# Output weights loaded into regions that the end of attention leaves, and split into slots of attention and the delta rule

## The chip, the cores and the metric

The kernel runs on one core of one Trainium2 chip. The metric is the time of one execution on the device in microseconds. The kernel before takes 645.64 us, the median of three runs (645.34 to 646.01).

The core's engines are TensorE (PE in the profile; PEld is its weight load), VectorE (DVE), ScalarE (ACT), GpSimd (POOL) and SyncE (SP), which issues nearly all transfers of this kernel.

## The reference

One decoder block on 1024 tokens of width 1024. After an RMS norm one projection feeds two groups of heads: eight heads of stick-breaking attention and four heads of a gated delta rule. Both results are normed by head, gated, joined and multiplied by one output weight; the residual is added and the result normed again.

```python
h = rmsnorm(x, norm1_w[layer])
proj = jnp.einsum('btd,de->bte', h, w_in[layer])
sb_q, sb_k, sb_v, sb_z, g_q, g_k, g_v, g_z, g_b, g_a = jnp.split(proj, split_idx, axis=-1)
...
o_sb = rmsnorm(o_sb.transpose(0, 2, 1, 3), sb_norm_w[layer]).reshape(b, t_len, SB_WIDTH)
o_sb = o_sb * jax.nn.silu(sb_z)
...
o_gdn = rmsnorm(o_gdn.transpose(0, 2, 1, 3), gdn_norm_w[layer]).reshape(b, t_len, GDN_WIDTH)
o_gdn = o_gdn * jax.nn.silu(g_z)
...
mixed = jnp.concatenate([o_sb, o_gdn], axis=-1)
x = x + jnp.einsum('bte,ed->btd', mixed, w_out[layer])
...
return rmsnorm(x, final_norm_w)
```

Rows 0 to 511 of `w_out` belong to the attention's half of `mixed`, rows 512 to 1023 to the delta rule's half.

## The kernel before, in words

Every float32 product is made of three products of rounded parts: an operand is split into a high half (a rounded copy, made by ACT) and a low half (what the rounding left, made by DVE or POOL), and high x high, high x low and low x high are added in PSUM (`mm3`).

**What sets the order.** The kernel is written as generators, called streams. A planner (`Model`, `interleave`) runs them against estimated costs while the program is built. Whenever the planned TensorE has nothing left, the ready stream of lowest number takes its next step, and what it records is appended to TensorE's order. The operations of the other four engines are put in the order in which the planner would start them: of those whose inputs are there, the one with the lowest priority value (`OUT_WEIGHTS` = -1 goes first, then `DELTA` = 0, `WEIGHTS` = 2, `BANK` = 5, `WINDOW` = 10, `OUTPUT` = 12, `RESULT` = 20). On the chip each engine then goes through its list strictly in that order. The planner counts for a 512 KB row 1.10 us before a transfer begins, 1.64 us for its bytes and 1.50 us until it has landed (`start`, `cost`), and a stream that waits for it goes on another 0.90 + 0.07 + 0.45 us later (`HOPS`, `TO_PE`, `SLACK`). Every operation goes through one recording helper, so all lines of the profile read L358; the groups are told apart by the names of their tiles.

**The stages around the change.** Attention runs head by head in four windows of 256 queries. In the last head, window w reads the region `sgw` of fixed memory (`sg1` 4 KB per partition, `sg2` 6 KB). A window makes its scores (from `q2`, `kh`, `kl`, with running products in `cc`), which sets `s7w`, then transposes and splits them (into `ahl`) and multiplies with `v2a`, which sets `e7w` and stores the result to `o_s`. The delta rule runs beside it: a chain of small steps (DVE `v`, `state` and `xct`, ACT `vr`) whose results go to `og_s`, and whose end sets `g`. The projections fill TensorE in between (stream number 100). The last of them are the gates z4 to z7 and z0 to z3, each in two halves of 512 columns: a PSUM bank `pp` (there are two), a sigmoid by ACT (`zs`), a product by DVE (`zt`, two buffers, shared under the tag `kt`) and a store to `gate_s`, which has the lowest priority. The end of the projections sets `proj`.

**The output weights (lines 1386 to 1422).** The output weight has eight rows of 128 x 1024 float32, 512 KB each. `weights_of` loads a raw row (`wor`), and splits it when it has landed: ACT makes the high half (`woh`) with the head norm's gain as scale, DVE the low half (`wol`). Two rows are in flight; the third load follows the split of the first. `out_weights` waits for `g`, closes the delta rule's pool, opens a pool `f0` in its place and makes weights 4 to 7 there, with the raw rows in three buffers that they share with the x rows of the first three blocks (tag `xr`). `out_weights_attention` waits for `proj`, closes the pool of the projections' input, opens `f1` there and makes weights 0 to 3 in it, with two raw buffers; then it loads the final norm's row `fnw`.

**The output stage.** For each block of 128 tokens, `enter_delta` (line 1446) loads the delta rule's result and gate into one of four buffers `kq` (`mgf` in the profile) and DVE scales it in four steps; it starts when pool `f0` is open, gate z7 is done and weights are there (`len(wts) > 1`). `prepare` (line 1472) turns a block by TensorE, multiplies it by the gate (DVE `mf`) and splits it (ACT `mh`, POOL `ml`; three buffers). `products_delta` multiplies it by weights 4 to 7, in two halves of 12 matmuls, each in a `pp` bank, and DVE adds the bank to the x row (`xr<-pp,xr`), which empties the bank; block b's end sets `db`. `enter_x` loads the x rows: the first three blocks into `f0`, the rest into `f1` once that is open. `enter_attention` (line 1513) does for the attention's blocks what `enter_delta` does, with the head norm (ACT `sq`, DVE `ssb`, POOL `rsb`, DVE `mgf<-mgf,rsb`); it waits for `f1`, for weight 3 and for the last delta input. `products_attention` follows the last delta block, and after each block ACT, DVE and POOL do the final norm (`yj`, `sy`, `ry`, `xr<-pc,fnw`, `xr<-po,fnw`) and SP stores the result.

Of the kernel before, what the change touches and what calls it, by code (L numbers as in the profile page):

```python
# [22 lines left out]
SBH = 8  # L23
# [12 lines left out]
OUT_WEIGHTS, DELTA, WEIGHTS, BANK, WINDOW, OUTPUT, RESULT, DECAYS = -1, 0, 2, 5, 10, 12, 20, 25  # L36
# [437 lines left out]
def block(tc, xT_d, x_d, n1_d, wE_d, wQ_d, wC_d, conv_d, alog_d, dtb_d, mixw_d, wo_d, fnw_d, out_d):  # L474
    nc = tc.nc
    ck = Model({"V": nc.vector, "A": nc.scalar, "G": nc.gpsimd, "P": nc.tensor, "S": nc.sync})
    V, A, G, TE, S = ck.V, ck.A, ck.G, ck.P, ck.S

    with ExitStack() as top:
        top.enter_context(tc.manual_schedule(engines={mybir.EngineType.PE}))  # L480

        def open_pool(name, space="SB", ctx=top, before=(), **kw):
            if space != "SB":
                kw["space"] = getattr(bass.MemoryType, space)
            return Pool(ck, ctx.enter_context(tc.tile_pool(name=name, bufs=1, **kw)), space, before)

        fx = Fixed(ck, nc, {**{f"sg{w}": (2048 * (w + 1), 1) for w in range(4)}, "o2": (1024, 1), "kq": (4096, 4)})
# [19 lines left out]
        mixw = cst.tile([P, NK], F32, name="mixw")  # L507
# [32 lines left out]
        at_ = open_pool("att", side="right")  # L540
# [140 lines left out]
        for b in range(NB):  # L681
            xr = s0.tile([P, T], F32, tag="xr", bufs=5, name="xr")
# [295 lines left out]
        def delta_load():  # L978
            yield lambda: "dec" in flags
            for h in range(GH):  # L980
                for g in range(2):
                    u = 2 * h + g
                    gst[h, g] = {}
                    half = "" if g else ".0"
                    yield lambda: u < 4 or f"c{u - 4}" in flags
                    if u > 3:
                        yield flags[f"c{u - 4}"]
                    kq = fx.tile([P, 4, 2, P], F32, "kq", "kq")
                    ts = slice(512 * g, 512 * g + 512)
# [300 lines left out]
        def attention_values():  # L1290
            yield lambda: "v1" in flags and "dec" in flags
            for h in range(SBH):
                yield lambda: h == 0 or f"e{h - 1}3" in flags
                hd["v", h] = v2 = at_.tile([P, NB, P], F32R, tag="v2a", name="v2a")
                flags[f"va{h}"] = S.dma_start(v2.bitcast(F32), v_s[:, :, h].rearrange("b s u d -> s b (u d)").bitcast(F32))
# [90 lines left out]
        wts = {}  # L1386
        pools = {}

        def weights_of(pool, ks, tag, bufs):
            ks = list(ks)  # L1390
            raws = {}

            def load(k):
                r = pool.tile([P, D], F32, tag=tag, bufs=bufs, name="wor")
                raws[k] = r, S.dma_start(r, wo_d[k * P:(k + 1) * P, :])

            for k in ks[:2]:
                load(k)
            for n, k in enumerate(ks):
                w, landed = raws[k]  # L1400
                yield landed
                wh, wl = [pool.tile([P, D], F32R, name=f"wo{c}{k}") for c in "hl"]
                A.activation(wh, w, AF.Copy, scale=mixw[:, k:k + 1])
                wts[k] = wh, wl, V.scalar_tensor_tensor(wl, w, mixw[:, k:k + 1], wh.bitcast(F32), ALU.mult, ALU.subtract)
                if n + 2 < len(ks):
                    load(ks[n + 2])

        def out_weights():
            yield lambda: "g" in flags
            gdn_ctx.close()  # L1410
            pools[0] = open_pool("f0", before=gd.ops())
            flags["pool0"] = True
            yield from weights_of(pools[0], range(4, 8), "xr", 3)

        def out_weights_attention():
            yield lambda: "proj" in flags and "pool0" in flags
            proj_ctx.close()
            pools[1] = open_pool("f1", before=px.ops(), side="right")
            flags["pool1"] = True
            yield from weights_of(pools[1], range(4), "wr", 2)  # L1420
            fnw = wts["fnw"] = pools[1].tile([P, D], F32, name="fnw")
            S.dma_start(fnw, fnw_d.partition_broadcast(P))

# [20 lines left out]
            return pools[0].tile([P, D], F32, tag="xr", bufs=3, name=name) if b < 3 else pools[1].tile([P, D], F32, tag="yr", bufs=5, name=name)  # L1444

        def enter_delta():
            yield lambda: "pool0" in flags and "z7" in flags and len(wts) > 1
            f0 = pools[0]
            for b in range(NB):
                yield lambda: fx.room("kq")  # L1450
                mg, mx, gt = block_inputs()
                S.dma_start(mx, og_s[b].rearrange("p h d -> p (h d)"))
                S.dma_start(gt, gate_s[4:8, :, b * P:(b + 1) * P].rearrange("k e t -> e k t"))
                ck.hold(mg)
                for g in range(GH):
                    gs = slice(g * P, (g + 1) * P)
                    r = V.tensor_scalar(mx[:, gs], mx[:, gs], rsg[:, g, b:b + 1], None, ALU.mult)
                ready["in", b, 1] = mg, gt, r
                yield
# [3 lines left out]
        def enter_x():  # L1463
            yield lambda: ("in", 0, 1) in ready
            for b in range(NB):
                yield lambda: b < 3 or "pool1" in flags
                xs_[b] = block_tile(b, "xr")
                S.dma_start(xs_[b], x_d[b * P:(b + 1) * P, :])
                ck.hold(xs_[b])
                yield  # L1470
# [62 lines left out]
        def products_attention():  # L1533
            yield lambda: f"d{NB - 1}" in flags
            for b in range(NB):
# [3 lines left out]
                for got in product(b, 0, parts):  # L1539
# [43 lines left out]
        pre = Stream(delta_pre(), 0.7, DELTA + 0.7)  # L1583
        interleave(ck, lambda: ps.room("pz", 4),
                   [Stream(delta_scan(), 0, DELTA), Stream(delta_solve(), 0.5, DELTA + 0.5), Stream(delta_substitute(), 0.6, DELTA + 0.6),
                    pre, Stream(delta_load(), 0.4, DELTA + 0.4), Stream(attention(), 9.995, WINDOW), Stream(attention_values(), 9.99, WINDOW), Stream(out_weights(), 9, OUT_WEIGHTS), Stream(out_weights_attention(), 9.25, OUTPUT + 1), Stream(enter_x(), 9.31, OUTPUT), fill,
                    Stream(enter_delta(), 9.3, OUTPUT), Stream(prepare(1), 9.2, OUTPUT), Stream(products_delta(), 101, OUTPUT),
                    Stream(enter_attention(), 9.1, OUTPUT - 3), Stream(prepare(0), 9.05, OUTPUT - 2), Stream(products_attention(), 102, OUTPUT - 1.5)])

# [37 lines left out]
```

## Time and profile before

| | |
|---|---|
| median of three runs | 645.64 us (645.34 to 646.01) |
| profiled execution | 647.36 us, its span 645.0 us, granted TensorE clock 0.998 |
| busy share of the span | PE 98%, PEld 84%, DVE 68%, ACT 61%, POOL 53% |
| last head's windows 1, 2, 3 issue the store of their result | 502.0, 508.8, 515.5 us |
| delta rule issues its last store | 521.5 us |
| raw rows of the output weights issued | 523.5 to 567.8 us |
| their low halves begun | 530.9 to 577.8 us |
| products with the output weights (first to last) | 542.9 to 638.3 us |
| DMA share, 500 to 520 us, 521 to 540 us, 540 to 545 us | 0.22, 0.81, 1.06 |

Times are microseconds from the start of the span unless ns is written. A line of the timeline gives start, duration, engine, operation, the tile written, the tiles read and the shapes; in brackets stands the time for which the engine was idle before it, and what it waited for. A group's line ends with its count, its busy time, the mean time of one, and the idle time before its members. SPq is SyncE's queue: such a line is the issue of a transfer, not the transfer. The ends of matmuls are modelled: their starts are what is exact, so a pace is read from start to start.

### The profile page before, as it was taken

To read this page: it belongs to the slowest core of one execution; us is meant where nothing else is said; L and a number is where in the kernel's file an instruction comes from. 1 tells how busy PE (TensorE), PEld (TensorE's weight loads), DVE (VectorE), ACT (ScalarE), POOL (GpSimd) and SP (SyncE) were. 2 spreads that over 40 slices of the span, in tenths; PEclk is the share of its full clock that TensorE was granted. 3 is DMA by queue.
4 is the path that set the end of the run, shared out by engine and by line. 5 is a ranking of instruction groups with operands and counts; after the bars stand their busy time and mean duration, and the time that the engine had idled before them with its cause. 6 is when DMAs were issued, how large, how long until landed. Compare 5 with 4: busy or idle time off the path is not lost.

```text
span 645.0 us, 11378 instructions
## 1 busy us (share of the span) xinstructions
PE 633.7 (98%) x3816; PEld 540.5 (84%) x3816; DVE 435.6 (68%) x810; ACT 392.6 (61%) x943; POOL 340.6 (53%) x429
## 2 busy tenths in 40 slices
PE   8999999999999999999999999999999999999996
PEld 7889988988888888888888788888888887888785
DVE  4359985133776797776877677667869527486874
ACT  5665467553876677856877766757578533222653
POOL 0125142964978487773569596477626131224742
PEclk9999999999999999999999999999999999999999
DMA  8968235886286352656254583444512259962323
GB/s 294 303 245 305 86 131 162 313 286 229 81 262 189 99 172 81 202 182 185 71 169 125 158 274 84 123 146 117 185 52 73 79 191 332 357 197 65 99 99 130
DMA packets 96633, 111.80 MB, mean 173 GB/s; under 512 B 28544, under 2 KB 61504, under 8 KB 96576
## 3 DMA queue, kind: packets, MB, share of 16 engines
q1 hardware_dynamic: 96288, 110.89, 52.2%
q8 instruction: 30, 0.49, 0.3%
q14 instruction: 27, 0.22, 0.1%
q10 hardware_dynamic: 288, 0.20, 0.1%
HBM read 76.03 MB, written 35.03 MB: 172 GB/s over the span
## 4 chain that ended last, share of the span: by engine, by line
PE 53%; POOL 3%; issue 2%; DVE 2%; DMA 1%; ACT 0%; POOLq 0%; SPq 0%
PE pp L358 34%; PE pz L358 13%; PE po L358 4%; PE pc L358 2%; DMA vt<-g_s 1%; POOL sgf L358 1%; POOL rsb L358 1%; POOL tt L358 0%; DVE xr L358 0%; POOL ac L358 0%; DVE cc L358 0%; POOL wel L358 0%; DVE ahl L358 0%; POOL ml L358 0%; POOL ry L358 0%
## 5 line engine op out<-in xcount | busy, mean ns | idle before, releaser
L358 PE MATMUL pp<-xh,weh 128*128 128x512 f32 x360 | 146.0, 406 | 0.0
L358 PE MATMUL pp<-xh,wel 128*128 128x512 f32 x360 | 141.2, 392 | 0.0
L358 PE MATMUL pp<-xl,weh 128*128 128x512 f32 x360 | 140.5, 390 | 0.0
L358 POOL TENSOR_TENSOR sgf<-sgf,cc 128x128 f32<-128x128 f32 (+3 forms) x64 | 77.3, 1210 | 48.0 <-DVE cc L358 46.7
L358 POOL TENSOR_TENSOR wel<-wer,weh 128x512 fp32r<-128x512 f32 x48 | 62.1, 1298 | 68.2 <-ACT weh L358 66.4
L358 PEld LDWEIGHTS pp<-xh,wel 128*128 128x128 f32 x360 | 67.5, 188 | 15.1
L358 PEld LDWEIGHTS pp<-xl,weh 128*128 128x128 f32 x360 | 67.8, 188 | 11.7
L358 PEld LDWEIGHTS pp<-xh,weh 128*128 128x128 f32 x360 | 67.7, 188 | 11.6
L358 DVE TENSOR_TENSOR_SCAN cc<-pz,step 128x384 f32<-128x384 f32 (+2 forms) x64 | 53.4, 847 | 13.7 <-ACT pz L358 7.5
L358 DVE TENSOR_TENSOR ahl<-pz,ahl 128x512 fp32r<-128x512 f32 (+1 forms) x80 | 50.0, 631 | 11.9 <-ACT ahl L358 11.5
L358 ACT ACTIVATE ahl<-pz 128x512 fp32r<-128x512 f32 (+1 forms) x80 | 44.0, 563 | 17.7 <-PE pz L358 17.4
L358 ACT ACTIVATE sgf<-pz,rs 128x384 f32<-128x384 f32 (+3 forms) x96 | 52.9, 593 | 1.5 <-PE pz L358 1.1
L358 PE MATMUL pp<-woh,mh 128*128 128x512 f32 (+2 forms) x132 | 52.1, 395 | 1.2 <-DVE xr L358 1.2
L358 ACT ACTIVATE pz<-pz,ns 128x384 f32<-128x384 f32 (+3 forms) x96 | 52.2, 577 | 0.0
L358 PE MATMUL pp<-woh,ml 128*128 128x512 f32 (+2 forms) x132 | 50.9, 385 | 0.0
L358 PE MATMUL pp<-wol,mh 128*128 128x512 f32 (+2 forms) x132 | 50.6, 384 | 0.0
L358 PE MATMUL po<-ahl,v2a 128*128 128x512 f32 (+1 forms) x160 | 49.0, 401 | 0.0
L358 POOL TENSOR_TENSOR ac<-ac,pre 128x512 f32<-128x512 f32 x24 | 30.9, 1291 | 30.8 <-ACT pre L358 24.2
L358 POOL TENSOR_TENSOR ml<-mf,mh 128x512 fp32r<-128x512 f32 x16 | 22.0, 1377 | 42.6 <-ACT mh L358 32.3
L358 DVE SCALAR_TENSOR_TENSOR pp<-pre,conv,pp 128x512 f32<-128x512 f32 x42 | 31.5, 749 | 18.3 <-ACT pp L358 18.0
L358 DVE TENSOR_TENSOR_SCAN cc<-pz,cc,step 128x512 f32<-128x512 f32 (+1 forms) x32 | 38.8, 1211 | 5.5 <-ACT pz L358 4.8
L358 PE MATMUL pz<-kh,q 128*128 128x384 f32 (+3 forms) x96 | 36.0, 381 | 0.2 <-DVE cc L358 0.2
(290 smaller groups left out, 1531.5 us busy)
## 6 DMA issues: line engine op xcount, KB each, us to landing
wer<-wE SPq DMA_DIRECT2D x48, 256.0 KB, 3.0
xr<-x SPq DMA_DIRECT2D x16, 512.0 KB, 7.4
g_s<-ac SPq DMA_DIRECT2D x24, 256.0 KB, 2.1
v_s<-v2e SPq DMA_DIRECT2D x16, 256.0 KB, 3.0
kqf<-g_s SPq DMA_DIRECT2D x16, 256.0 KB, 3.4
v2a<-v_s SPq DMA_DIRECT2D x8, 512.0 KB, 5.9
q<-qk_s SPq DMA_DIRECT2D x8, 512.0 KB, 4.0
kh<-qk_s SPq DMA_DIRECT2D x8, 512.0 KB, 3.9
```

What stands on the lines that cost most here:

```text
L358: ins = f(*args, **kw).ins
```

## The change

The eight raw rows no longer go through buffers of the two late pools. A new stream, `out_rows`, loads them into the fixed regions `sg1` and `sg2` in turn, in the order 4, 5, 6, 7, 0, 1, 2, 3: the first once the last head's scores are done and its window 1 is through, the second after window 2, every further one when the row before it in that region has been split. Its loads have the highest priority. `out_weights` splits rows 4 to 7 into slots that attention leaves (`kh` and `kl`; `q2` and one `cc`; the other `cc` and `v2a`; both `ahl`), two of them after the scores, two after the last window; it no longer waits for the delta rule. `out_weights_attention` opens `f0` when the delta rule is done and splits rows 0 to 3 there, with a low priority. `out_rest` opens `f1` when the projections are done, as before, and loads the final norm's row after the second delta block. `enter_delta` no longer waits for weights.

```diff
-        def weights_of(pool, ks, tag, bufs):
-            ks = list(ks)
-            raws = {}
-
-            def load(k):
-                r = pool.tile([P, D], F32, tag=tag, bufs=bufs, name="wor")
+        raws = {}
+
+        def out_rows():
+            yield lambda: f"s{SBH - 1}3" in flags and f"e{SBH - 1}1" in flags
+            for n, k in enumerate((4, 5, 6, 7, 0, 1, 2, 3)):
+                if n == 1:
+                    yield lambda: f"e{SBH - 1}2" in flags
+                if n > 1:
+                    yield lambda: fx.room(f"sg{1 + n % 2}")
+                r = fx.tile([P, D], F32, "wor", f"sg{1 + n % 2}")
+                ck.hold(r)
                 raws[k] = r, S.dma_start(r, wo_d[k * P:(k + 1) * P, :])
-
-            for k in ks[:2]:
-                load(k)
-            for n, k in enumerate(ks):
-                w, landed = raws[k]
-                yield landed
-                wh, wl = [pool.tile([P, D], F32R, name=f"wo{c}{k}") for c in "hl"]
-                A.activation(wh, w, AF.Copy, scale=mixw[:, k:k + 1])
-                wts[k] = wh, wl, V.scalar_tensor_tensor(wl, w, mixw[:, k:k + 1], wh.bitcast(F32), ALU.mult, ALU.subtract)
-                if n + 2 < len(ks):
-                    load(ks[n + 2])
+                yield
+
+        def weight(k, wh, wl):
+            w = raws[k][0]
+            A.activation(wh, w, AF.Copy, scale=mixw[:, k:k + 1])
+            wts[k] = wh, wl, V.scalar_tensor_tensor(wl, w, mixw[:, k:k + 1], wh.bitcast(F32), ALU.mult, ALU.subtract)
+            ck.free(w)
 
         def out_weights():
+            places = [(t, 2 if t in ("cc", "ahl") else 1) for t in ("kh", "kl", "q2", "cc", "cc", "v2a", "ahl", "ahl")]
+            for n, k in enumerate(range(4, 8)):
+                yield lambda: k in raws and (n < 2 or f"e{SBH - 1}3" in flags)
+                yield raws[k][1]
+                weight(k, *[at_.tile([P, D], F32R, tag=t, bufs=m, name="wo") for t, m in places[2 * n:2 * n + 2]])
+                yield
+
+        def out_weights_attention():
             yield lambda: "g" in flags
             gdn_ctx.close()
-            pools[0] = open_pool("f0", before=gd.ops())
+            f0 = pools[0] = open_pool("f0", before=gd.ops())
             flags["pool0"] = True
-            yield from weights_of(pools[0], range(4, 8), "xr", 3)
-
-        def out_weights_attention():
+            for k in range(4):
+                yield lambda: k in raws
+                yield raws[k][1]
+                weight(k, *[f0.tile([P, D], F32R, name=f"wo{c}{k}") for c in "hl"])
+                yield
+
+        def out_rest():
             yield lambda: "proj" in flags and "pool0" in flags
             proj_ctx.close()
             pools[1] = open_pool("f1", before=px.ops(), side="right")
             flags["pool1"] = True
-            yield from weights_of(pools[1], range(4), "wr", 2)
+            yield lambda: "d1" in flags
             fnw = wts["fnw"] = pools[1].tile([P, D], F32, name="fnw")
             S.dma_start(fnw, fnw_d.partition_broadcast(P))
...
         def enter_delta():
-            yield lambda: "pool0" in flags and "z7" in flags and len(wts) > 1
+            yield lambda: "pool0" in flags and "z7" in flags
...
-Stream(out_weights(), 9, OUT_WEIGHTS), Stream(out_weights_attention(), 9.25, OUTPUT + 1), Stream(enter_x(), 9.31, OUTPUT), fill,
+Stream(out_rows(), 9.1, OUT_WEIGHTS), Stream(out_weights(), 9, OUT_WEIGHTS), Stream(out_weights_attention(), 9.25, OUTPUT + 1), Stream(out_rest(), 9.26, OUTPUT + 1), Stream(enter_x(), 9.31, OUTPUT), fill,
```

More of the change, by code (lines that the diff above doesn't have):

```diff
@@ L1585, in block @@
                    [Stream(delta_scan(), 0, DELTA), Stream(delta_solve(), 0.5, DELTA + 0.5), Stream(delta_substitute(), 0.6, DELTA + 0.6),
-                    pre, Stream(delta_load(), 0.4, DELTA + 0.4), Stream(attention(), 9.995, WINDOW), Stream(attention_values(), 9.99, WINDOW), Stream(out_weights(), 9, OUT_WEIGHTS), Stream(out_weights_attention(), 9.25, OUTPUT + 1), Stream(enter_x(), 9.31, OUTPUT), fill,
+                    pre, Stream(delta_load(), 0.4, DELTA + 0.4), Stream(attention(), 9.995, WINDOW), Stream(attention_values(), 9.99, WINDOW), Stream(out_rows(), 9.1, OUT_WEIGHTS), Stream(out_weights(), 9, OUT_WEIGHTS), Stream(out_weights_attention(), 9.25, OUTPUT + 1), Stream(out_rest(), 9.26, OUTPUT + 1), Stream(enter_x(), 9.31, OUTPUT), fill,
                     Stream(enter_delta(), 9.3, OUTPUT), Stream(prepare(1), 9.2, OUTPUT), Stream(products_delta(), 101, OUTPUT),
```

## The prediction

> **What bounds the kernel now.** I read the engine shares first, then the chain that ended last, then the waits of TensorE in the last 105 us, and last the timeline around the two places that those waits point to.
>
> ```profile
> span 645.0 us, 11378 instructions
> PE 633.7 (98%) x3816; PEld 540.5 (84%) x3816; DVE 435.6 (68%) x810; ACT 392.6 (61%) x943; POOL 340.6 (53%) x429
> ```
>
> TensorE (PE) is busy for 98% of the span. Since the ends of its matmuls are modelled, busy alone does not say that it issues as fast as it can. The chain of waits says more, because it merges matmuls that follow each other without a pause:
>
> ```profile
> 521.09 18.41 PE pp L358 x81
> ...
> 546.86 0.70 DVE xr L358
> 547.60 3.02 PE pp L358 x12
> ...
> 574.34 12.36 PE pp L358 x54
> ```
>
> 81 matmuls in 18.41 us are 227 ns each, 54 in 12.36 us are 229 ns. The first stretch is the last two gate projections, the second the output product of the delta rule. They run at one pace, though different data and a different amount of DMA traffic lie beside them. So from 521 us on TensorE works at a steady pace that this change does not touch: the same matmuls, with the same operand shapes, remain. What can be won there is its pauses, and the waits of TensorE from 540 us to the end name only these:
>
> ```profile
> PE pp L358 <- DVE xr L358: 1.2, 2, 0.8
> ```
>
> Two pauses, 1.2 us together, both waits for VectorE (DVE) to empty a PSUM bank. Their exact price comes from the starts of the matmuls around them:
>
> ```profile
> 546.43 0.39 PE L358 MATMUL pp<-woh,ml 128*128 128x512 f32 x1
> 547.60 0.50 PE L358 MATMUL pp<-woh,mh 128*128 128x512 f32 x1 [0.78 <-DVE xr L358]
> ...
> 602.92 0.39 PE L358 MATMUL pp<-woh,ml 128*128 128x512 f32 x1
> 603.72 0.47 PE L358 MATMUL pp<-woh,mh 128*128 128x512 f32 x1 [0.41 <-DVE xr L358]
> ```
>
> Start to start is 1.17 us and 0.80 us where 0.227 is the pace, so 0.94 us and 0.57 us are lost, 1.51 us together. Before 502 us the change moves nothing (its first gate opens with the attention's last windows, below). So 1.51 us is close to the most that it can win, unless the whole order behind 502 us turns out better in some way that this trace doesn't show.
>
> Here a rule of the Trainium skill speaks against my bound: "Perfetto Trace Analysis", section "Identifying the Most-Contended Engine", holds matmul busy time for a bad measure and weight-load busy time for a good one. By the 84% of the page about 103 us of the span would be headroom. The 81 matmuls without a pause show none that a move of transfers could use, so the measurement decides and the bound stands.
>
> **The loads.** The change keeps eight raw rows of 512 KB, and their eight splits, and moves them.
>
> ```profile
> L358 SPq DMA_DIRECT2D wor<-wo x8: 327/333/652, 523.5 to 567.8; - x8
> L358 ACT ACTIVATE woh<-wor,mixw x8: 1136/1140/1157, 529.7 to 573.9; 128x1024 fp32r<-128x1024 f32 x8
> L358 DVE SCALAR_TENSOR_TENSOR wol<-wor,mixw,woh x8: 1274/1280/1867, 530.9 to 577.8; 128x1024 fp32r<-128x1024 f32 x8
> DMA to landing us min/median/max: 3.2/4.2/7.0
> ...
> 497.20 2.00 POOL L358 TENSOR_TENSOR sgf<-sgf,cc 128x1024 f32<-128x1024 f32 x1 [0.40 <-DVE cc L358]
> 502.03 0.37 SPq L358 DMA_DIRECT2D o_s<-oe  x1
> 508.78 0.38 SPq L358 DMA_DIRECT2D o_s<-oe  x1
> 515.48 0.37 SPq L358 DMA_DIRECT2D o_s<-oe  x1
> ```
>
> The last head's scores end at 499.2 and its windows 1, 2 and 3 store their results at 502.0, 508.8 and 515.5. These are the gates. So row 4 can be issued at about 502, row 5 at about 509, row 6 when the split of row 4 has emptied its region (502 + 4.2 + 1.14 + 1.28, but behind row 5: 509), row 7 at about 516, and rows 0 to 3 one by one at some 4 us each from 518 on. The last split is then done near 537, where it was done at 579.7 (577.8 + 1.9). SyncE's (SP) queue gets none more to issue, 8 x 0.33 us as before. Each is moved past what SP carries from 502 to 522: the stores of the delta rule's scan, the result stores of the attention and the weight loads of the last gate tiles. A row that waits for its region holds those. I price this at nothing, because the stores' results are first wanted when the products begin (543, below), and
>
> ```profile
> 503.27 0.86 SPq L358 DMA_DIRECT2D wer<-wE  x2
> ...
> 513.21 0.62 ACT L358 ACTIVATE weh<-wer 128x512 fp32r<-128x512 f32 x1
> ...
> L358 SPq DMA_DIRECT2D og_s<-goe x8: 319/320/333, 487.3 to 521.5; - x8
> ```
>
> a gate weight issued at 503.3 is first read at 513.2; with 4.2 us to land (the raw row's time, for twice the size), the cover is 5.7 us. If that cover went, TensorE would wait for each us beyond it.
>
> **The splits.** Four of them (rows 0 to 3) leave the stretch 552 to 580: 4 x 1.14 = 4.6 us of ScalarE (ACT) and 3 x 1.28 + 1.87 = 5.7 us of DVE. Three (4 to 6) enter the stretch 500 to 520 and the others 520 to 537:
>
> ```profile
> 500.00:520.00 20.00, 20.00 (x125) 17.46 (x125) 10.03 (x24) 9.57 (x28) 4.04 (x5) 1.00 0.22 69
> ...
> L358 DVE TENSOR_TENSOR_SCAN cc<-pz,cc,step 128x512 f32<-128x512 f32 (+1 forms) x32 | 38.8, 1211 | 5.5 <-ACT pz L358 4.8
> ...
> 592.00:604.00 12.00, 11.59 (x57) 9.27 (x56) 10.36 (x16) 6.00 (x12) 9.50 (x7) 1.00 0.39 119
> ```
>
> (The windows give the busy time of PE, PEld, DVE, ACT and POOL, then clock, DMA share and GB/s.) DVE goes from 10.0 to 13.9 of 20 us there, ACT from 9.6 to 13.0. The splits of rows 4 to 7 have the highest order of all in the planner, so up to 1.3 us at a time they go ahead of the delta rule's steps (v, state, xct, vr). The scan's last store is issued at 521.5 and its product starts at 543, so 21 us of gate projections cover this: 0, unless TensorE's fixed order stands behind a step that came late. Between nothing and the price in the second rival I take nothing: the nearest row is the attention's own scan, as long, which goes between the same steps now.
>
> **What starts earlier.** The delta rule's inputs no longer wait for two split weights, and weight 3, for which the attention's inputs wait, is ready sooner:
>
> ```profile
> 528.81 0.45 SPq L358 DMA_DIRECT2D mgf<-og_s  x1
> ...
> 566.48 1.28 DVE L358 SCALAR_TENSOR_TENSOR wol<-wor,mixw,woh 128x1024 fp32r<-128x1024 f32 x1
> 567.78 0.33 SPq L358 DMA_DIRECT2D wor<-wo  x1
> ...
> 568.69 0.38 SPq L358 DMA_DIRECT2D mgf<-o_s  x1
> ```
>
> The first goes from 528.8 to about 523.5, the second (now held by SP behind the raw row, which waits for the split of 566.48) to about 555, when the second delta block is done (543.1 + 48 x 0.227 = 554). The final norm's row waits for that block too; it is first used by the first finished output block, near 600, so this costs nothing.
>
> **The first pause.** The product's second half wants a PSUM bank that the last gate tile still holds:
>
> ```profile
> 538.05 0.40 SPq L358 DMA_DIRECT2D gate_s<-zt  x1
> 543.14 0.39 PE L358 MATMUL pp<-woh,mh 128*128 128x512 f32 x1
> 543.39 0.60 ACT L358 ACTIVATE zs<-pp 128x512 f32<-128x512 f32 x1 [2.21 <-PE pp L358]
> ...
> 547.82 0.69 DVE L358 TENSOR_TENSOR mf<-pz,mgf 128x512 f32<-128x512 f32 x1 [0.28 <-POOL ml L358]
> 548.43 0.68 DVE L358 TENSOR_TENSOR zt<-pp,zs 128x512 f32<-128x512 f32 x1
> ...
> 540.00:545.00 5.00, 5.00 (x26) 4.11 (x25) 5.00 (x14) 1.23 (x2) 1.54 (x1) 1.00 1.06 379
> ...
> xr<-x SPq DMA_DIRECT2D x8, 512.0 KB, 7.5
> wor<-wo SPq DMA_DIRECT2D x2, 512.0 KB, 7.0
> ```
>
> The bank's sigmoid is done at 544.0, its second step zt runs at 548.4. Two things hold zt: its two buffers, one of which waits for a store that SP issued only at 538.05, behind loads; and the input scalings of the delta blocks, which fill DVE from 540 to 545. DMA is at its limit there (share 1.06), with eight x rows and two raw rows issued between 536 and 552. In the change the two raw rows are gone from this stretch, three x rows can be issued ahead of it with the first blocks' inputs, 5 us earlier, and the scalings come earlier too. zt then follows its sigmoid: 544.0 + 0.69 = 544.7, and the second half wants its bank at 543.1 + 12 x 0.227 = 545.9 (block transposes that move ahead of the products shift both alike). I take the whole 0.94.
>
> **The second pause.** It lies in the DVE-heavy stretch 592 to 604 (10.36 of 12 us):
>
> ```profile
> 596.70 0.15 DVE L358 TENSOR_SCALAR ssb<-ssb 128x8 f32<-128x8 f32 x1
> 599.77 1.29 POOL L358 TENSOR_TENSOR ml<-mf,mh 128x512 fp32r<-128x512 f32 x1
> 600.03 1.05 DVE L358 TENSOR_SCALAR ssb<-ssb 128x8 f32<-128x8 f32 x1
> ```
>
> With the attention's inputs 13 us earlier, their scaling no longer piles up on the first finished output blocks, so this may go. But a tiny step took 1.05 us instead of 0.15 while GpSimd (POOL) ran beside it, and that pair can meet again wherever the pile ends up. Between 0 and 0.57 I take half, 0.28.
>
> "SBUF: State Buffer", section "Who interferes with whom", of the Trainium skill states that VectorE and GpSimd share one pair of ports as an exclusive lock. The trace agrees (1.05 against 0.15). By that rule alone this pause would stay, and the sum would be 0.94.
>
> **The sum.** 0.94 + 0.28 = 1.22 us, bounds 0.94 and 1.51. The profiled execution took 647.36 us (2.36 of them outside its span), 1.72 more than the median of 645.64, so I take the difference alone to the median: 644.4, or 0.19%. A measurement of this kernel can tell about 0.2% (1.29 us, to 644.35) from no change, so this forecast lies on that line.
>
> **Rivals.** First, the pause moves and nothing is won. The saturated stretch stays: five of eight x rows (512 KB) still can't be issued until the projections end, at 543, and they alone are 2.6 MB, 7 us at the 379 GB/s reached. A DVE that waits in order for a late input holds zt or xr behind it as now. For it: DMA share 1.06. Against: 1 MB of raw rows less in that stretch. Time 645.6 (one such wait of 0.94 stays, one of 0.28 comes for the one that went).
>
> Second, slower: ACT, in order, stands in front of a raw row that hasn't landed, between 504 and 523, and TensorE's order, written for an earlier arrival, stands with it. The planner counts 4.24 us to landing and waits 1.42 more, so it decides when a landing takes over 5.66 us. The longest of the trace is 7.0: 1.34 us for each late row. With three late ones 4.0 us, less the 0.94 won: 648.7; with two, 647.4. Behind ACT's split wait vr, the copies of the attention and the gate sigmoid, for which DVE and then TensorE wait. Against it: DMA share is 0.22 there, and the 7.0 was seen at 1.06.
>
> Third, the change doesn't do what it says: the splits of rows 6 and 7 wait for the last window (515.5), and the rest for the end of the scan (522). If regions come free late, rows 0 to 3 stay in the busy stretch: 645.6.
>
> **Chances.** Forecast 0.50; of it 0.28 beyond 0.2%, since both pauses may go whole. First rival 0.26, second 0.15 (0.13 of it beyond 0.2%), third 0.05; 0.04 for a larger gain than the pauses allow. Faster 0.28 + 0.04 = 0.32; same 0.22 + 0.26 + 0.02 + 0.05 = 0.55; slower 0.13. The range goes down to both pauses (644.13) less half of the spread of the three runs (645.34 to 646.01, 0.33), 643.8, and up to one late row with nothing won, 645.64 + 1.34 = 647.0; with the 0.04 below and two or more late rows above (about 0.1), some 0.14 is left out.
>
> **What would show it.** Right: raw rows issued from 502 on, splits done before 540, zt less than 2 us behind its sigmoid, no wait of TensorE for xr near 547, the attention's first input before 560, fewer than 10.4 us of DVE in the 12 us at the first finished outputs. Wrong: a pause of TensorE between 502 and 523 that ends with ACT's vr or ahl (second rival), an unchanged 0.78 near 547 (first), splits after 545 (third), or a change of pace of the gapless matmuls from 227 ns, which would overturn the bound itself.

## The result, and the profile after

The changed kernel takes 644.59 us, the median of 20 executions (644.20 to 645.19), beside 645.83 us for the kernel before on the same chip (645.34 to 646.26). The ratio is 0.998, with a 95% interval of 0.9974 to 0.9987: 1.24 us are gone, where 1.22 were forecast. The profiled execution took 645.19 us, 2.03 of them outside its span.

The page of the changed kernel, its first part:

```profile
span 643.2 us, 11380 instructions
## 1 busy us (share of the span) xinstructions
PE 633.8 (99%) x3816; PEld 540.3 (84%) x3816; DVE 435.3 (68%) x810; ACT 392.4 (61%) x943; POOL 339.9 (53%) x429
```

Each engine carries the work that it carried before, within 0.7 us (POOL 339.9 for 340.6); the span is shorter by 1.8 us. So no engine got less to do. What went is, in the main, idle time of TensorE. Its waits from 540 us to the end name nothing any more (the list is empty), and the timeline of its matmuls shows the two places at which it paused before. The columns are start, duration, engine, line, operation and tiles:

```profile
543.03 0.63 PE L358 MATMUL pp<-wo,mh 128*128 128x512 f32 x2
...
545.60 0.39 PE L358 MATMUL pp<-wo,ml 128*128 128x512 f32 x1
545.83 0.63 PE L358 MATMUL pp<-wo,mh 128*128 128x512 f32 x2
...
602.79 0.40 PE L358 MATMUL pp<-woh,ml 128*128 128x512 f32 x1
603.02 0.40 PE L358 MATMUL pp<-woh,mh 128*128 128x512 f32 x1
...
636.51 0.28 PE L358 MATMUL pp<-woh,ml 128*128 128x192 f32 x1
```

Where 1.17 us lay between two starts there are now 0.23 (545.60 to 545.83), and where 0.80 lay there are 0.23 (602.79 to 603.02). From the first matmul of the output product to the last it is 636.51 - 543.03 = 93.48 us. The kernel before has its first there at 543.14 (shown above) and its last at 638.34:

```profile
638.34 0.28 PE L358 MATMUL pp<-woh,ml 128*128 128x192 f32 x1
```

That is 95.20 us, so the stage is 1.72 us shorter. But the two stretches don't hold the same matmuls, 456 before and 448 after. The difference is the transposes of two blocks (`pz<-step,mwf`, four to a block). Before, they stand between the products, and in the changed kernel ahead of the first of them, since the inputs come earlier. Before and after:

```profile
544.53 0.47 PE L358 MATMUL pz<-step,mwf 128*128 128x128 f32 x4
545.60 0.46 PE L358 MATMUL pz<-step,mwf 128*128 128x128 f32 x4
...
533.42 0.46 PE L358 MATMUL pz<-step,mwf 128*128 128x128 f32 x4
534.48 0.45 PE L358 MATMUL pz<-step,mwf 128*128 128x128 f32 x4
```

What leaves the stage makes the stretch ahead of it longer. Attention's store of a result just ahead of the change (`o_s<-oe`) is issued at 498.19 before and 497.35 after, and from there to the first product it is 44.95 and 45.68 us, 0.73 more. So like for like the stage is 0.99 us shorter, and from that store to the end of the span it is 1.00 (146.81 and 145.81), beside 1.24 between the medians. The other 0.84 us of the two spans' difference were lost ahead of the change, where before's profiled execution waited 1.29 us for a transfer near 366 us and the changed kernel's 0.61.

The two pauses went whole, 0.94 + 0.57 = 1.51 us, and part of this was paid back, because the pace changed. The twelve products from 543.03 to 545.83 above come every 233 ns. Over the 192 products of the delta rule's half, the starts lie 232.8 ns apart in the mean from product to product (pauses and transposes left out), where it was 228.4 before: 192 x 4.4 ns = 0.84 us. 1.51 - 0.84 is 0.67, which leaves 0.32 in pieces too small to name.

Why the first pause went is seen on DVE. Before, its timeline reads

```profile
541.63 3.47 DVE L358 TENSOR_SCALAR mgf<-mgf,rsg 128x128 f32<-128x128 f32 x12
545.09 0.69 DVE L358 TENSOR_TENSOR mf<-pz,mgf 128x512 f32<-128x512 f32 x1
```

and after

```profile
543.92 0.69 DVE L358 TENSOR_TENSOR zt<-pp,zs 128x512 f32<-128x512 f32 x1 [2.87 <-ACT zs L358]
544.53 0.87 DVE L358 TENSOR_SCALAR mgf<-mgf,rsg 128x128 f32<-128x128 f32 x4
546.03 0.69 DVE L358 TENSOR_TENSOR xr<-pp,xr 128x512 f32<-128x512 f32 x1 [0.63 <-PE pp L358]
```

The twelve input scalings that stood there are four, and DVE sat idle for 2.87 us until the sigmoid ended. `zt` comes right behind it, at 543.92 instead of 548.43, and the bank is free before the second half of the product wants it. The stretches by engine of the changed kernel (PE, PEld, DVE, ACT, POOL, then clock, DMA share and GB/s):

```profile
500.00:520.00 20.00, 20.00 (x122) 17.32 (x121) 13.00 (x27) 11.94 (x29) 4.13 (x5) 1.00 0.60 184
...
540.00:545.00 5.00, 5.00 (x24) 4.08 (x23) 1.77 (x5) 2.27 (x3) 1.61 (x2) 1.00 1.08 371
592.00:604.00 12.00, 12.00 (x59) 9.89 (x58) 8.55 (x15) 5.53 (x12) 6.30 (x5) 1.00 0.34 98
```

DVE went from 5.00 to 1.77 of 5 us at the first pause, and from 10.36 to 8.55 of 12 us at the second, while the DMA share at the first stayed as it was (1.06 and 1.08). The rows, splits and inputs, grouped by tile (duration min/median/max in ns, first and last start):

```profile
L358 SPq DMA_DIRECT2D worf<-wo x8: 328/332/448, 500.6 to 538.3; - x8
L358 ACT ACTIVATE wo<-worf,mixw x4: 1139/1142/1145, 505.8 to 522.1; 128x1024 fp32r<-128x1024 f32 x4
L358 DVE SCALAR_TENSOR_TENSOR wo<-worf,mixw,wo x4: 1273/1278/1286, 507.8 to 523.2; 128x1024 fp32r<-128x1024 f32 x4
L358 DVE SCALAR_TENSOR_TENSOR wol<-worf,mixw,woh x4: 1269/1276/1279, 528.8 to 553.4; 128x1024 fp32r<-128x1024 f32 x4
DMA to landing us min/median/max: 3.7/5.0/6.4
...
L358 SPq DMA_DIRECT2D mgf<-og_s x8: 319/354/504, 522.8 to 550.1; - x8
L358 SPq DMA_DIRECT2D mgf<-o_s x8: 319/320/320, 556.1 to 597.6; - x8
```

`wo` are the splits of rows 4 to 7, which the delta rule's half of the product reads, done at 524.5; `wol` those of rows 0 to 3, done only at 554.7.

### The profile page after: what moved, and what is told of

Its sections match the earlier page's. It is cut to its first block, busy times and chain, and to the rows that moved or that the text cites. A ratio compares the mean times of both kernels' runs of the same rounds, so it can differ in the third digit from the quotient of the medians.

```text
span 643.2 us, 11380 instructions
## 1 busy us (share of the span) xinstructions
PE 633.8 (99%) x3816; PEld 540.3 (84%) x3816; DVE 435.3 (68%) x810; ACT 392.4 (61%) x943; POOL 339.9 (53%) x429
## 4 chain that ended last, share of the span: by engine, by line
PE 91%; POOL 3%; DMA 2%; DVE 1%; issue 1%; ACT 1%; POOLq 0%; SPq 0%; ACTq 0%
PE pp L358 54%; PE pz L358 26%; PE po L358 7%; PE pc L358 3%; DMA vt<-g_s 1%; DMA o_s<-oe 1%; POOL wel L358 1%; POOL ac L358 1%; DMA n<-n 1%; DVE cc L358 0%; POOL tt L358 0%; POOL tm L358 0%; POOL sgf L358 0%; POOL xs L358 0%; DVE ahl L358 0%
## 5 line engine op out<-in xcount | busy, mean ns | idle before, releaser
L358 PE MATMUL pp<-wo,mh 128*128 128x512 f32 x128 | 40.7, 399 | 0.0
L358 DVE TENSOR_TENSOR xr<-pp,xr 128x512 f32<-128x512 f32 (+2 forms) x33 | 22.2, 672 | 19.3 <-PE pp L358 18.8
L358 PEld LDWEIGHTS pz<-step,stf 128*128 128x128 f32 x288 | 30.9, 140 | 4.8
```

Source lines behind the costliest of these rows:

```text
L358: ins = f(*args, **kw).ins
```

## The experiments

In each trace the stage from the first to the last matmul of the output product was taken, and what lies between the last matmul and the end of the span:

| kernel | ratio to before (95%) | first matmul, us | last | stage | matmuls in it | to the end |
|---|---|---|---|---|---|---|
| before | 1 | 543.14 | 638.34 | 95.20 | 456 | 6.66 |
| after | 0.9980 (0.9974 to 0.9987) | 543.03 | 636.51 | 93.48 | 448 | 6.65 |
| e1, before, delta inputs early | 1.0021 (1.0012 to 1.0031) | 541.89 | 638.61 | 96.72 | 448 | 6.94 |
| e2, before, gate stores first | 1.0073 (1.0061 to 1.0086) | 541.26 | 641.30 | 100.04 | 456 | 6.66 |
| e3, before, attention inputs early | 1.0005 (0.9997 to 1.0014) | 541.59 | 636.46 | 94.87 | 456 | 7.55 |
| e4, before, all three | 1.0019 (1.0008 to 1.0030) | 541.41 | 636.67 | 95.26 | 448 | 6.67 |
| e5, after, delta inputs late | 1.0017 (1.0009 to 1.0026) | 542.12 | 637.36 | 95.24 | 448 | 7.31 |
| e6, after, rows 0 to 3 late | 0.9988 (0.9980 to 0.9997) | 544.04 | 637.50 | 93.46 | 448 | 6.74 |
| e7, after, all rows late | 1.0033 (1.0021 to 1.0046) | 542.38 | 640.35 | 97.97 | 448 | 6.65 |
| e8, after, planner told sooner | 0.9996 (0.9987 to 1.0005) | 542.43 | 635.89 | 93.46 | 448 | 7.56 |
| e9, e8 padded | 0.9985 (0.9976 to 0.9994) | 542.93 | 636.39 | 93.46 | 448 | 7.09 |
| e10, e3 padded | 0.9995 (0.9986 to 1.0004) | 542.18 | 637.03 | 94.85 | 456 | 7.08 |
| e11, after padded | 0.9985 (0.9977 to 0.9994) | 542.93 | 636.41 | 93.48 | 448 | 7.08 |

A stage compares only with one of as many matmuls: before's 95.20 stands for 95.20 - 0.73 = 94.47 among those of 448. Without a pause the stage is 93.46 to 93.48 in five kernels (after, e6, e8, e9 and e11).

The pace falls into two groups as well. In the seven kernels that split rows 4 to 7 into slots of attention (after, e5 to e9 and e11), the products of the delta rule's half come every 233 ns (median), and in the six others every 227. The attention's half, whose weights lie in a late pool, has 227 in all thirteen. So the pace goes with the slots and costs each of the seven some 0.84 us. What it is in the slots that slows a matmul was not tested.

**Theory and rivals.** The theory was that of the prediction: two pauses, the first undone by the delta rule's inputs going early, the second by the attention's. The rivals: that one of the conditions behind these steps is the cause by itself, so that one changed line of the kernel before would win the same; and that only the loading matters. e1 to e4 change a condition of the kernel before and leave the loading as it was; e5 to e7 undo one part of the change each.

### e1: the delta rule's inputs early, rows as before

```diff
-            yield lambda: "pool0" in flags and "z7" in flags and len(wts) > 1
+            yield lambda: "pool0" in flags and "z7" in flags
...
-            yield lambda: ("in", 0, 1) in ready
+            yield lambda: ("in", 0, 1) in ready and len(wts) > 1
```

The second line, in `enter_x`, keeps the x rows where they were.

> The kernel before, with the delta blocks' inputs no longer waiting for split weights (the x rows still wait as before, since they share buffers with the raw rows). Theory (the first pause is zt, held behind the input scalings and behind a late store): the scalings go ahead of 540, but the store of the tile before is still behind loads in SP's order, so the pause near 547 shrinks without being sure to go: 645.83 less 0 to 0.94, 645.3. Rival (the raw rows' traffic between 523 and 560 makes the pause): the pause stays at 0.94 and the time at 645.8. The second pause (0.57 near 603) stays in both.

It took 646.83 us beside 645.21. Its waits of TensorE from 540 us on (us in total, times, longest):

```profile
PE pp L358 <- DVE wol L358: 1.4, 2, 1.2
PE pp L358 <- ACT woh L358: 0.3, 1, 0.3
```

and the stretch behind them, by engine as above:

```profile
546.00:550.00 4.00, 3.77 (x10) 2.67 (x9) 2.47 (x3) 1.15 (x1) 0.00 (x0) 0.57 0.96 375
```

The wait for `xr` is gone, since `zt` runs at 542.7, and against the expectation the second pause is gone too (the attention's first input leaves at 562.7, 568.7 before). In their place the product stands before its own weights: the inputs, issued at 518.7, overtake the raw rows, and the first split is at 533.4 instead of 529.7. The condition `len(wts) > 1` was there for a reason, and dropped by itself it loses. Behind the pauses the granted clock is 0.57, told of below.

### e2: stores of the last gate tiles first

```diff
+                ck.prio, prio = (OUT_WEIGHTS if i in (2, 3) else ck.prio), ck.prio
-                return S.dma_start(gate_s[i, :, hs], zt)
+                r = S.dma_start(gate_s[i, :, hs], zt)
+                ck.prio = prio
+                return r
```

> The kernel before, with the stores of the last two gate tiles at the highest priority in place of the lowest. Theory: zt gets its buffer early, but the planner still places the scalings ahead of it where they are ready; the pause near 547 goes or halves: 645.0 to 645.4. Rival (traffic): zt's buffer is no matter, 645.8. The second pause stays.

It took 649.91 us, the slowest of all. The wait for `xr` near 547 is gone, so the store that held the buffer was a cause of the first pause. But TensorE now waits at 588 to 593. The longest of its waits is

```profile
PE pp L358 <- ACT mh L358: 2.0, 1, 2.0
```

SP's timeline shows what came late:

```profile
556.13 16.92 SPq L358 DMA_DIRECT2D wor<-wo  x2
573.10 0.42 SPq L358 DMA_DIRECT2D fnw<-fnw  x1
573.57 0.42 SPq L358 DMA_DIRECT2D mgf<-o_s  x1
```

and the stretch behind the wait, by engine, is

```profile
592.00:598.00 6.00, 5.50 (x16) 4.24 (x16) 3.88 (x7) 1.89 (x3) 3.51 (x3) 0.51 0.29 92
```

SP stood at the last raw row, which waits for the split that frees its buffer, and the attention's first input left at 573.57 (568.69 before). Its block was wanted when the delta rule's products ended, near 588. So the 4.9 us by which that input came later were more than the old loading had to spare.

### e3: the attention's inputs early, rows as before

```diff
-            yield lambda: "pool1" in flags and "z3" in flags and 3 in wts
+            yield lambda: "pool1" in flags and "z3" in flags
```

> The kernel before, with the attention blocks' inputs no longer waiting for weight 3. Theory (the second pause comes from the attention's inputs piling up on the first finished blocks): first input near 560 in place of 568.7, the pause near 603 goes, the one near 547 stays: 645.83 - 0.57 = 645.3. Rival (the second pause is the port held by POOL, wherever the steps stand): the pause stays or moves: 645.8.

The first pause stays, as the one wait left shows:

```profile
PE pp L358 <- DVE xr L358: 0.8, 1, 0.8
```

The second is no longer named, but it isn't gone: the product behind a block's transposes starts 0.55 us after the first of them (601.60 and 602.15), where 0.30 is usual (544.53 and 544.83 before). So 0.25 us of 0.57 are left. The edit moved the attention's first input alone (556.9); the second left at 567.6 (569.6 before), behind the last raw row. The stage is 0.33 us shorter, which is that difference, but what follows the last matmul is 0.89 longer, so the time, 645.42 beside 645.21, shows no gain. The end is taken up at e8.

### e4: all three at once

> The kernel before with the edits of the three runs beside it together; raw rows and splits stay where they were. Theory (the gain is the two pauses, however they go): 645.83 - 0.94 - 0.57 = 644.3, as the changed kernel within 0.3. Rival (moving the raw rows is what gains, by traffic or by the splits that leave 552 to 580): 645.3 to 645.8.

Its edit is those of e1, e2 and e3 together. Its waits are, to the tenth, those of e1 (`wol` 1.4, `woh` 0.3), and the time is 645.77 (645.27 to 648.54). That is 0.56 us over the kernel before, worse than even the rival had it. With every condition set free but the rows loaded as before, nothing is won: 95.26 us of stage, 0.79 over the 94.47 that before has of the same matmuls. The rows must come first.

### e5: the changed kernel, delta inputs held back

```diff
-            yield lambda: "pool0" in flags and "z7" in flags
+            yield lambda: "pool0" in flags and "z7" in flags and len(wts) > 5
```

> The changed kernel, with the delta blocks' inputs (and with them the x rows) held until six weights are recorded, some 10 us later; the rows and splits stay as changed. Theory (a bank of the last gate tile is emptied late when the input scalings fill VectorE after 540, so both moves are needed, weights and inputs): a pause of about 0.9 near 545 returns, time 0.9 over the changed kernel, 1.2 - 0.9 = 0.3 under the kernel before (ratio 0.9995). Rival (moving the raw rows out of the traffic is enough): no pause returns, ratio 0.998 as the changed kernel.

It took 646.76 us beside 645.82. The inputs left at 528.8, the time of the kernel before, and the waits are back:

```profile
PE pp L358 <- DVE xr L358: 1.4, 2, 0.8
```

Both now lie at the start of the product (behind 544.68 and 548.96), 0.95 and 0.74 us lost, with `zt` at 549.6. These two, and not the one that was forecast, make the stage 1.76 us longer than the changed kernel's. Behind the last matmul there are 0.66 us more, of which 0.36 lie ahead of DVE's last `sy`. So early rows alone bring nothing: it took 0.94 us more than the kernel before, since the pauses are back and the slower pace stays. The gain of the early rows is that the delta rule's inputs may go early without e1's loss.

### e6: the changed kernel, rows 0 to 3 held back

```diff
-                    yield lambda: fx.room(f"sg{1 + n % 2}")
+                    yield lambda: fx.room(f"sg{1 + n % 2}") and (n < 4 or "proj" in flags)
```

> The changed kernel, with the raw rows 0 to 3 held until the projections end (near 543); rows 4 to 7 stay early. Theory (rows 0 to 3 matter only by holding the attention's inputs until weight 3 is recorded, and by their traffic): no pause near 545, but the attention's first input goes back to 565 or later and the second pause (0.3 to 0.6 near 600) returns; ratio 0.9985 to 0.999. If the held inputs come later than the products, as in the run with the store first, a pause of 2 us or more near 590 and a lower clock behind it: ratio over 1.002. Rival (rows 4 to 7 are all that counts): ratio 0.998.

It took 644.79 us beside 645.82, 0.9988 (by luck in the range of the theory, and with an interval that overlaps the changed kernel's), and no wait of TensorE is left; the stage is 93.46. The theory, by which early rows 0 to 3 undo the second pause, failed here. Their splits came at 551.7 to 570, later than in the changed kernel, and the attention's first input still left at 557.3. Early rows 4 to 7 are enough.

### e7: the changed kernel, all rows held until the scan's end

```diff
-            yield lambda: f"s{SBH - 1}3" in flags and f"e{SBH - 1}1" in flags
+            yield lambda: f"s{SBH - 1}3" in flags and f"e{SBH - 1}1" in flags and "g" in flags
```

> The changed kernel, with all raw rows held until the delta rule's scan has ended (near 522), so that they load where the kernel before loads its first four, through the fixed regions two at a time. Theory (the early weights are what lets the inputs go early): the inputs' and x rows' traffic now stands beside the rows', weights 6 and 7 come after 543, and the products wait for them as in the run with early inputs alone: 1 to 2 us of pause near 545; ratio 1.000 to 1.003. Rival (the slots, not the early time, are what counts): ratio 0.998.

It took 647.35 us beside 645.82. Its waits of TensorE:

```profile
PE pp L358 <- DVE wo L358: 1.6, 2, 0.8
PE pp L358 <- ACT wo L358: 0.4, 1, 0.4
```

and the splits of rows 4 to 7, by tile:

```profile
L358 DVE SCALAR_TENSOR_TENSOR wo<-worf,mixw,wo x4: 1281/1283/1287, 526.8 to 546.1; 128x1024 fp32r<-128x1024 f32 x4
```

The last of these splits starts at 546.1, 3.7 us after the product's first matmul, where the changed kernel has it at 523.2. The pauses lose 0.54, 1.09 and 0.98 us from start to start, and behind them the clock falls here too, to 0.61 in 547 to 551. The start of the loads inside the attention's last windows is what the change needs, and the other slots and regions win nothing by themselves.

### e8: the changed kernel, planner told that rows land 3 us sooner

```diff
-            self.at(self.dma + 1500, self.finish, op)
+            self.at(self.dma + 1500 - op.rush, self.finish, op)
...
-                yield
+                raws[k][1].rush = 3000; yield
```

`rush` is 0 for every other transfer, and 3000 ns for the eight raw rows.

> The changed kernel, with the planner told that every raw row lands 3 us sooner than it does, so ScalarE's order has each split that much earlier. The prediction's second rival says what a late row costs: ScalarE stands for 3 - 1.42 = 1.6 us in front of each row that lands as slowly as the planner otherwise counts, with the delta rule's steps behind it, and TensorE pays for those that it needs at once. Theory (the pauses of ScalarE lie under the gate projections): TensorE's order has other matmuls only until the next step of the scan, so some of it shows: 1 to 3 us over the changed kernel, ratio 1.000 to 1.003. Rival (all of it is covered): ratio 0.998.

This asks for the prediction's second rival: TensorE's order is now written for rows that come 3 us before they do. ACT waits 1.5 us for them and TensorE not once; the splits move to 503.7 to 516.8, and the stage is 93.46. A split written that much too early is covered. Yet the time is 645.47 us beside 645.82, 0.9 above the changed kernel, and the trace has it all behind the last matmul: 7.56 us instead of 6.65. The transfers of the last stores, with their us to landing at the end of each row:

```profile
out<-yf SPq DMA_DIRECT2D x1, 320.0 KB, 3.3
out<-yf ACTq DMA_DIRECT2D x1, 192.0 KB, 3.5
```

and, of the queues from 639.5 to 642.2 us, the one beside the two that carry the stores (packets, MB, share of 16 engines):

```profile
q14 instruction: 1, 0.01, 0.7%
```

One packet of 8 KB in the queue that fetches instructions lies between the packets of the last store (at 640.90, the store from 639.8 to 642.1). In e3, the other kernel whose last stores took 3.3 and 3.5 us, it is the same (at 641.46). In all the rest they took 2.4 and 2.6, and no fetch lies there.

### e9, e10 and e11: the same kernels, padded

To move the fetches without touching the work, six tiny instructions were put at the start of each of DVE, POOL and ACT, with values that no later step uses:

```diff
+        [(nc.vector.memset(root, 0.5), nc.gpsimd.memset(ns8, 0.0)) for _ in range(6)]
+        [nc.scalar.activation(rs8, ns8, AF.Copy) for _ in range(6)]
         V.memset(root, 0.5)
```

> The kernel of e8 with six tiny instructions more on each of DVE, ACT and POOL at the very start (under 1 us, before the first product), which move the place at which an engine's next piece of instructions is fetched. Theory: the 0.9 us by which e8 ended later than the changed kernel is the fetch that fell inside its last store; moved out of it, that store lands in 2.4 to 2.6 us instead of 3.3 to 3.5, the tail from the last matmul to the end goes from 7.56 to about 6.65, and the ratio from 0.9996 to about 0.998. Rival: the tail has nothing to do with the fetch; it stays near 7.5 and the ratio near 0.9996, or rises by what the padding costs.

> The kernel of e3 with the same padding. Theory: tail from 7.55 to about 6.65, ratio from 1.0005 to about 0.9992, so that the second pause alone is worth its 0.5 us. Rival: tail and ratio unchanged.

> The changed kernel with the same padding. Theory: its last store, which no fetch touched, stays so if the fetch that stood 3 us ahead of it moves further ahead: tail 6.65, ratio 0.998; should the fetch land inside the store, tail about 7.5 and ratio 0.9994. Rival: tail 6.65 wherever the fetch falls.

The landing answers as the theory has it. Of e9:

```profile
out<-yf SPq DMA_DIRECT2D x1, 320.0 KB, 2.4
out<-yf ACTq DMA_DIRECT2D x1, 192.0 KB, 2.6
```

The fetch of e9 is at 638.56, ahead of the store, and e10's two stores take 2.4 and 2.6 us as well, its fetch now at 638.89. With the stage unchanged, e9 took 644.81 us beside 645.79, much like e11, the changed kernel with the same padding, at 644.77. (Its one profiled span, 643.48, doesn't show this beside e8's 643.45, because its product began 0.50 us later. The medians do, with intervals that overlap.) But the end came back only half way: 7.09, 7.08 and 7.08 us in the three, where 6.65 was expected. The 0.43 us left lie after the last store's last packet (641.80 to the end at 643.48 in e9, 1.68 us; 641.92 to 643.16 in the changed kernel, 1.24), in e11 too, whose stores were never disturbed. That stretch isn't the same without padding either: it is 1.24 or 1.25 us in five kernels, some 1.35 in e3, e6 and e8, and 1.54 in e1 and e5. Why is not known. In e10 the time moved from 0.21 us above the kernel before (e3) to 0.38 below it, with intervals that overlap.

## Why the prediction held, and where its steps failed

**The bound.** Right that the pauses are what could be won there, and wrong in the step "a steady pace that this change does not touch: the same matmuls, with the same operand shapes, remain". The shapes remained, but half of the products now read their weights from attention's slots, and these come every 233 ns. The prediction named a change of pace from 227 ns as the sign that would overturn the bound. It came in small and cost some 0.84 us, a term that the sum doesn't have. The kernel before gives a hint of it: where two of attention's score matmuls (`pz<-kh,q`, `pz<-kl,q`) of 512 columns follow each other, the starts lie 232 to 234 ns apart in the mean. They are few and lie between other work, so it is no more than a hint.

**The first pause, 0.94.** Right in place and size, and `zt` less than a microsecond behind its sigmoid, as asked for. Its causes were both real: e2 removes it by the store, e1 by the inputs, and e5 brings it back by holding them. Of the reasons given, the saturated transfers were the weak one: it went while the DMA share stayed as it was.

**The second pause, half of 0.57.** The step "I take half" was mis-sized: it went whole. That the forecast 1.22 us came out beside the measured 1.24 is luck: 0.29 too little for this pause and 0.32 in small pieces stand against the 0.84 that the slower pace costs, which gives 0.99 in the profiled executions. The reason given, the attention's inputs, isn't shown: e3, with the first of them early, keeps 0.25 us of the pause, but e7, where the first two left at 571.0 and 572.4, later than before, has none of it.

That the pause would stay by the rule on ports was cited beside it: the Trainium skill, "SBUF: State Buffer", section "Who interferes with whom". The collision is still there: the changed kernel's step at 600.65 took 1.66 us and its like 0.69, while GpSimd ran `ml` from 600.47 on:

```profile
595.48 0.69 DVE L358 TENSOR_TENSOR mgf<-mgf,rsb 128x512 f32<-128x512 f32 x1 [1.19 <-POOL rsb L358]
...
600.65 1.66 DVE L358 TENSOR_TENSOR mgf<-mgf,rsb 128x512 f32<-128x512 f32 x1
```

So the trace agrees with the rule, and not with what was drawn from it: with 1.8 us less on DVE's list in these 12 us, no `xr` that TensorE needs stands late behind that collision.

**The loads, "the last split is then done near 537".** Wrong: 554.7. Rows 0 to 3 went one by one, the last issued at 538.3, and their splits gave way to other work. It cost nothing, because (e6) these four rows aren't needed early.

**Weight 3, "for which the attention's inputs wait, is ready sooner".** Right as a time of the input (556.1, asked for before 560), wrong as a need: e6 has the weight late (its split starts at 568.9) and the input nearly as early.

**What starts earlier.** Right: 522.8 for 523.5, and e5 shows that it is this step that pays.

**The rivals.** The first, that the pause moves and nothing is won, didn't happen here, but in e4 (it moves to the weights) and e5. The second didn't happen, and its condition didn't arise: the 6.4 us to landing, beyond the 5.66 from which it was to decide, was that of row 1, issued at 525.9, and ACT waited for none of rows 4 to 7. e8 is what asks for it, and there "TensorE's order, written for an earlier arrival, stands with it" failed: ACT stood 1.5 us for rows and TensorE for none, so the work queued between covers as much. The third didn't happen for rows 4 to 7, and for rows 0 to 3 it half did, without harm.

## What to carry to other kernels

A condition that holds a transfer back may be all that keeps another transfer in time: freed by itself (e1, e2, e4) it lost up to 0.7%, and the early load behind it paid only together with it. In a kernel whose main engine is 98% busy, add up its pauses from start to start before forecasting, and read what stood in the list of the engine that it waited for, more than the load of the queues. Compare the stage that was changed, but count its instructions first: here eight transposes that moved out of it made 0.73 of 1.72 us. Read the pace again where operands get a new place, though their shapes stay. And look at the end of the trace by itself, where 0.9 us can come or go with the work unchanged.

## What the runs showed of the hardware

**Half the clock can follow pauses of some 1.4 us and less.** In e1 TensorE's starts near 545 lie 0.73, 1.66 and 0.63 us apart; behind them the granted clock is 0.57 in 546 to 550, and matmuls come 0.43 us apart for about 3 us:

```profile
545.44 0.50 PE L358 MATMUL pp<-wol,mh 128*128 128x512 f32 x1 [1.16 <-DVE wol L358]
...
547.23 0.63 PE L358 MATMUL pp<-woh,ml 128*128 128x512 f32 x1
547.66 0.63 PE L358 MATMUL pp<-woh,mh 128*128 128x512 f32 x1
```

e4 has the same pauses, and there the same stretch was granted 1.00: 95.26 us of stage for 96.72, so the halved clock cost 1.46 us on top of the 2.3 that the pauses lose. This may be why the executions of these two spread so far (645.37 to 648.04 us in e1, 645.27 to 648.54 in e4; no other kernel's lie more than 1.9 apart), but only one execution of each was profiled. Pauses of 0.95 and 0.74 us, 4 us apart in e5, left the clock at 1.00. The Trainium skill, "TensorE: Matmul & The Clock Gate", section "Part 1: The HAM clock gate (the "warmup" mystery)", has a clock of full or half speed, set by how busy TensorE was in a free-running window of 3.4 us. The half speed, and that equal pauses ended differently, agree with it. Its section "Why this matters for your kernels" warns of gaps of over some 3 us; here the longest from start to start was 1.66, and the trace decides.

**The pace of a matmul went with the place of its operand.** With the same shapes, products that read a weight from attention's slots came every 233 ns and those that read it from a late pool every 227, in thirteen kernels without an exception. The cause stays open.

**An instruction fetch inside the last store** costs that store 0.9 us to landing (3.3 and 3.5 for 2.4 and 2.6), shown by e3, e8 and their padded forms.
